# Differential attention with a plain float32 value product, and two query blocks sharing the end of their chain

## The chip, the cores and the metric

The kernel runs on one core of one Trainium2 chip. The metric is the device time of one execution in microseconds (us). A core has five engines that matter here: TensorE (PE, matrix products; PEld is its weight load), VectorE (DVE), ScalarE (ACT), GpSimd (POOL) and SyncE (SP), whose queue issues nearly all DMA transfers. PE writes its results to PSUM, 8 banks of 2 KB for each of 128 partitions; DVE and ACT read them from there, POOL cannot.

## The reference

One encoder layer over 1024 rows of width 1024, in float32: half a SwiGLU step, then two token mixers in parallel (a chunked band attention A with 8 heads, and a differential attention B with 4 heads), gated and merged, then another half SwiGLU step and a norm. The change lies in mixer B:

```python
def diff_attention(q, k, v, t5_table, lam, lambda_init, subln_g):
    ...
    def block(args):
        qblk, bi = args
        ...
        sc = jnp.einsum('bqhrd,bkhrd->bhrqk', qblk, k).astype(jnp.float32) * scale
        ...
        p = jax.nn.softmax(sc, axis=-1)
        attn = p[:, :, 0] - lam * p[:, :, 1]
        return jnp.einsum('bhqk,bkhe->bqhe', attn.astype(v.dtype), v)

    o = lax.map(block, (qblocks, jnp.arange(nqb)))
    o = o.transpose(1, 0, 2, 3, 4).reshape(b, s, h, 2 * d)
    o = rms_norm(o, subln_g) * (1.0 - lambda_init)
    return o.reshape(b, s, h * 2 * d)
```

Each head has two score matrices (r = 0, 1), one value matrix of width 128, and a norm over its 128 outputs. A block of 128 queries sees the keys of its own and earlier chunks.

## The kernel before

**Split products.** PE multiplies operands of type float32r in one pass, at less than float32 accuracy. Almost every product is therefore written as a sum of products of two parts: `split` (L94) rounds a tile to float32r on ACT (`hi`, L97 or, with a scale, L99) and subtracts on DVE (`lo`, L102 or L104), and `mm3` (L126) adds hi x hi, hi x lo and lo x hi. Transposes by PE, and the product at L958, use plain float32 operands.

**Stages.** The first SwiGLU step, then the mixer's input projection (among it `project_v`, L665, which makes the values of both mixers with a seven-product scheme), then both attentions, then the merge, the output projection, and the second SwiGLU step. Intermediate results go through DRAM.

**Projection of the values.** For each of eight results per mixer, `sink` (L673) splits two tiles of 128 rows and 256 columns into hi and lo columns lying side by side, and stores them in `v_d`. For mixer B a head's 256 columns are its 128 hi and its 128 lo columns.

**Attention.** `run` (L811) goes through all jobs, first 32 of A (`jobs_a`), then 32 of B (`jobs_b`: 4 heads of 8 query blocks). A job is a generator: each step of `run` starts one job and moves the four jobs before it to their next `yield`, latest first. A job of B does this:

- Block start: at a head's first job, `load_qkv` (L757) loads queries, keys, exchanged keys and values, 1 MB each, into tiles of the pool `big` (14 buffers, where also the eight outputs `y` of all heads stay). At every second head the bias rows of two heads are loaded too (`bias_rows`, L798, eight DMAs into one tile `nb`).
- Scores for r = 0 and 1 (L779, L780: hi and lo of the keys), bias and row minimum on DVE (L787), exponential and row sum on ACT (L789). Two reciprocals (L922, L924), each into a one-column tile `ri` of a pool with four buffers. L925 makes the weight of the second softmax, L927 the combined probabilities. The first reciprocal, `r1`, is used again at the end.
- Two steps later: up to four 128 x 128 transposes into one PSUM tile `pt` (L795), split into hi and lo (L97, L102).
- One step later: the product with the values. For each block of 128 keys, L943 multiplies the hi probabilities with the 256 columns (hi and lo values), L944 the lo probabilities with the 128 hi columns. ACT scales the two halves by `r1` (L946, L948), POOL adds them (L949). DVE sums the squares (L952), POOL takes the power -1/2 (L139) and scales the identity by it (L955).
- One step later: a plain product of the output with that diagonal transposes and norms it (L958), and `split` with the gain `gsub` (L99, L104) writes the two parts of `y`.

After every second job of B a `filler` (`branch_a`, L881) runs one step: twelve products of 512 columns (L128 to L130) for A's output projection, with a gate tile `gl` loaded from DRAM, one product on DVE (L892) and a store (L893).

The order of each engine's instructions is worked out by the framework from the program's order and its own model of times (`schedule_with_timeline_sim=True`). Each engine, and SP's queue, then keeps that order. A tile that finds no free buffer in its pool waits until one is released.

## Time and profile before

| | |
|---|---|
| time, median of 3 runs | 2154.29 us (2150.46 to 2155.05) |
| span of the profiled execution | 2151.1 us |
| mean granted clock of PE | 0.994 |
| DMA moved in the span | 333.55 MB, mean 155 GB/s |
| stretch of mixer B's softmax and products | from about 1182 to 1353 us |

The page gives the profiled execution by its span, from first to last instruction; the time of a run is taken around it, and the median of the runs is 3.2 us above this span.

How to read the profile: `L943` is line 943 of the kernel. `pv<-vt,whi` names the tile written and those read. A group's row gives line, engine, operation, tiles, shape and count, then the busy time in us and the mean of one in ns, then how long the engine stood idle just before the group's instructions and on whom it waited most. A row of the order of time gives start, duration, engine, line, operation, tiles and count, with the idle time before it in brackets. A row of waits gives who waited for whom, the sum in us, how often, and the longest. Durations of products overlap, since PE takes up the next product while the last one drains, so the pace is read from their starts.

### The profile page before, as it was taken

How to read it: one execution, taken by the hardware profiler on the slowest of the kernel's cores; microseconds unless marked ns; L12 is line 12 of the kernel's file. 1: busy time of each engine (PE TensorE's matmuls, PEld its weight loads, DVE VectorE, ACT ScalarE, POOL GpSimd, SP SyncE). 2: the span in 40 equal slices, each digit the busy share in tenths (PEclk: the TensorE clock that was granted, in tenths of full speed). 3: DMA queues.
4: the chain of work that ended last, by engine and by line, in shares of the span. 5: the costliest groups of instructions: out<-in, count | busy, mean ns of one | idle time of the engine just before them, and what ended most of it. 6: DMA issues, size and time to landing. Idle time of an engine off the chain costs nothing.

```text
span 2151.1 us, 29100 instructions
## 1 busy us (share of the span) xinstructions
PE 2080.7 (97%) x10073; PEld 1738.7 (81%) x10073; DVE 1442.3 (67%) x2650; ACT 980.2 (46%) x1919; POOL 181.4 (8%) x282
## 2 busy tenths in 40 slices
PE   6999999999999999999999988999999999999997
PEld 5788888888888788899788877788788888888886
DVE  7666566677577756566488977558766656658566
ACT  5433333334446544444498665146433333334444
POOL 2120000000001000000066233001000000000001
PEclk9999999999999999999999999999999999999999
DMA  6653333294445544553683364634543333366334
GB/s 194 173 169 111 95 96 120 93 327 143 117 128 162 168 142 164 198 196 136 230 275 105 136 211 133 233 119 151 172 156 95 111 96 95 114 237 228 98 117 158
DMA packets 277555, 333.55 MB, mean 155 GB/s; under 512 B 15404, under 2 KB 167996, under 8 KB 277408
## 3 DMA queue, kind: packets, MB, share of 16 engines
q1 hardware_dynamic: 276080, 327.94, 46.7%
q0 software_dynamic: 1184, 3.24, 0.6%
q8 instruction: 79, 1.29, 0.3%
q14 instruction: 68, 0.56, 0.1%
q10 hardware_dynamic: 144, 0.52, 0.1%
HBM read 226.45 MB, written 105.19 MB: 154 GB/s over the span
## 4 chain that ended last, share of the span: by engine, by line
PE 82%; DVE 6%; DMA 4%; ACT 3%; issue 2%; SPq 1%; POOL 0%; ACTq 0%; DVEq 0%; POOLq 0%
PE prod L128 18%; PE prod L129 18%; PE prod L130 18%; PE po L129 7%; PE po L128 7%; PE po L130 7%; DVE wlo L102 2%; PE pb L128 1%; PE pb L130 1%; PE pb L129 1%; ACT pm L789 1%; DMA raw<-in_ffn_w_in_dram 1%; ACT whi L97 1%; PE tr L205 1%; PE pt L795 1%
## 5 line engine op out<-in xcount | busy, mean ns | idle before, releaser
L129 PE MATMUL po<-wlo,whi 128*128 128x512 f32 x744 | 290.6, 391 | 2.2 <-DVE wlo L102 2.2
L130 PE MATMUL po<-whi,wlo 128*128 128x512 f32 x744 | 289.4, 389 | 0.0
L97 ACT CAST whi<-raw 128x512 fp32r<-128x512 f32 x200 | 124.3, 622 | 308.1 <-PE prod L129 238.3
L97 ACT CAST whi<-B 128x512 fp32r<-128x512 f32 x186 | 115.8, 623 | 272.0 <-PE po L129 265.4
L97 ACT CAST whi<-T 128x512 fp32r<-128x512 f32 x192 | 119.4, 622 | 244.2 <-PE prod L129 224.7
L102 DVE TENSOR_TENSOR wlo<-B,whi 128x512 fp32r<-128x512 f32 x186 | 128.0, 688 | 139.3 <-ACT whi L97 139.2
L113 DVE TENSOR_TENSOR c<-prod,c 128x512 f32<-128x512 f32 x190 | 131.1, 690 | 133.6 <-PE prod L130 121.1
L102 DVE TENSOR_TENSOR wlo<-raw,whi 128x512 fp32r<-128x512 f32 x200 | 137.0, 686 | 106.6 <-ACT whi L97 64.0
L128 PE MATMUL po<-whi 128*128 128x512 f32 x744 | 201.5, 390 | 0.0
L102 DVE TENSOR_TENSOR wlo<-T,whi 128x512 fp32r<-128x512 f32 x192 | 131.8, 687 | 92.1 <-ACT whi L97 90.8
L129 PEld LDWEIGHTS po<-wlo,whi 128*128 128x128 f32 x744 | 139.6, 188 | 33.7 <-DVE wlo L102 5.1
L139 POOL TENSOR_TENSOR r<-v,neg_half 128x1 f32<-128x1 f32 x64 | 49.7, 780 | 1383.0 <-DVE v L180 1264.7
L130 PEld LDWEIGHTS po<-whi,wlo 128*128 128x128 f32 x744 | 139.7, 188 | 28.7
L128 PEld LDWEIGHTS po<-whi 128*128 128x128 f32 x744 | 139.1, 188 | 28.8 <-ACT whi L97 0.2
L102 DVE TENSOR_TENSOR wlo<-N,whi 128x512 fp32r<-128x512 f32 x64 | 44.1, 689 | 113.6 <-PE prod L129 62.9
L102 DVE TENSOR_TENSOR wlo<-ha,whi 128x512 fp32r<-128x512 f32 x154 | 105.4, 684 | 9.0 <-ACT whi L97 9.0
L272 ACT COPY c<-prod 128x512 f32<-128x512 f32 x186 | 103.1, 586 | 11.2 <-DMA hA<-c 4.4
L97 ACT CAST whi<-ha 128x512 fp32r<-128x512 f32 x154 | 94.8, 615 | 16.9 <-PE prod L129 11.4
L789 ACT ACTIVATE pm<-pm,mn 128x640 f32<-128x640 f32 (+7 forms) x128 | 94.0, 736 | 11.8 <-DVE ri L924 6.1
L128 PE MATMUL prod<-S1h,whi 128*128 128x512 f32 x240 | 94.4, 393 | 2.4 <-ACT S1h L97 1.4
L787 DVE CUSTOM_DVE_ANT_0 pm<-sc,nb 128x640 f32<-128x640 f32 (+7 forms) x128 | 87.9, 698 | 11.4 <-PE sc L780 8.8
L128 PE MATMUL prod<-S2h,whi 128*128 128x512 f32 x240 | 94.0, 392 | 1.3 <-ACT whi L97 1.3
(237 smaller groups left out, 5338.9 us busy)
## 6 DMA issues: line engine op xcount, KB each, us to landing
raw<-in_ffn_w_in_dram SPq DMA_DIRECT2D x98, 512.0 KB, 4.3
raw<-in_w_mix_in_dram SPq DMA_DIRECT2D x47, 512.0 KB, 4.4
ha<-hS SPq DMA_DIRECT2D x88, 256.0 KB, 2.6
hA<-c SPq DMA_DIRECT2D x66, 256.0 KB, 4.2
ha<-hA SPq DMA_DIRECT2D x66, 256.0 KB, 2.7
B<-in_ffn_w_out_dram SPq DMA_DIRECT2D x12, 1024.0 KB, 10.2
hS<-hs SPq DMA_DIRECT2D x44, 256.0 KB, 2.7
hS<-c SPq DMA_DIRECT2D x44, 256.0 KB, 4.4
```

The costliest lines, as they stand in the source:

```text
L97: nc.scalar.copy(out=hi, in_=src)
L102: (nc.gpsimd if on_pool else nc.vector).tensor_tensor(out=lo, in0=src, in1=h, op=ALU.subtract)
L113: nc.vector.tensor_tensor(out=out_, in0=a, in1=b, op=op)
L128: nc.tensor.matmul(ps, a[0], b[0], start=first, stop=False, skip_group_check=shared)
L129: nc.tensor.matmul(ps, a[0], b[1], start=False, stop=False, skip_group_check=shared)
L130: nc.tensor.matmul(ps, a[1], b[0], start=False, stop=last, skip_group_check=shared)
L139: nc.gpsimd.tensor_tensor(out=r, in0=v, in1=neg_half, op=ALU.pow)
L205: nc.tensor.transpose(tr[:, k, :], rows[:, k * P:(k + 1) * P], ident)
L272: nc.scalar.copy(out=self.held[name], in_=p)
L787: nc.vector.tensor_tensor_reduce(out=d3, in0=sc, in1=nb.rearrange("p (n w) -> p n w", n=n), scale=1.0, scalar=3e38, op0=ALU.add, op1=ALU.m ...
L789: nc.scalar.activation(out=dst, in_=dst, func=AF.Exp, bias=mn, scale=-1.0, accum_out=rs)
L795: nc.tensor.transpose(pt[:, b, :], p, ident)
```

## The change

The values of mixer B stay plain float32, 128 columns a head, and one tile holds two heads. The transposed probabilities are copied by ACT in place of being split. One plain float32 product per block of keys takes the place of L943 and L944, and one scaling takes the place of L946, L948 and L949. Two consecutive query blocks write their outputs, sums of squares and diagonals into shared tiles; the power, the diagonals, the transposing products and the split run once for the two, in the job of the odd block. The two row sums of a job share a tile, and so do their reciprocals, which are taken in one instruction. The values of a head pair are loaded once, at the pair's first head, behind its keys and ahead of its bias rows, as before; the pair's second head loads none. Mixer A's loads keep their order.

```diff
-    v_d = drams(2, [S, 2 * HALF], "v", F32R)
+    va_d = dram.tile([S, 2 * HALF], F32R, name="va")
+    vb_d = dram.tile([S, HALF], F32, name="vb")
...
                 def sink(th, blk, ap):
+                    t0 = 4 * th + 2 * a
+                    if br == 1:
+                        if (th, blk) == (1, 0):
+                            o = temp([P, 2, 256], "vo")
+                            nc.scalar.copy(out=o, in_=ap)
+                            ap = o
+                        nc.sync.dma_start(out=vb_d[t0 * P:(t0 + 2) * P, blk * 256:(blk + 1) * 256].rearrange(
+                            "(s p) c -> p s c", p=P), in_=ap)
+                        return
...
+        def load_v(src, n, dtype):
+
+            vt = big([P, NT, 256], "vt", dtype)
+            move(nc.sync, vt, src.rearrange("(t p) c -> p t c", p=P)[:, :, n * 256:(n + 1) * 256])
+            return vt
...
-        def transpose_p(blocks):
+        def transpose_p(blocks, whole=False):
...
-            return split_units(pt[:, :len(blocks), :].rearrange("p b q -> p (b q)"))
+            src = pt[:, :len(blocks), :].rearrange("p b q -> p (b q)")
+            if not whole:
+                return split_units(src)
+            dst = sb.tile(list(src.shape), F32, tag="w", bufs=WU, name="pT")
+            nc.scalar.copy(out=dst, in_=src)
+            return dst
...
                     if hb % 2 == 0:
-                        nbs.append(big([P, 2, S], "nb", F32))
+                        nbs.append((big([P, 2, S], "nb", F32), load_v(vb_d, hb // 2, F32)))
                         for hh in range(2):
-                            bias_rows(nbs[-1][:, hh, :], diag_b, hb + hh, EB, WB)
-                    ctx_["nb"] = nbs[-1][:, hb % 2, :]
+                            bias_rows(nbs[-1][0][:, hh, :], diag_b, hb + hh, EB, WB)
+                    ctx_["nb"] = nbs[-1][0][:, hb % 2, :]
+                    ctx_["vt"] = nbs[-1][1][:, :, (hb % 2) * P:(hb % 2 + 1) * P]
...
-                pr, rs = [], []
+                pr, rs = [], small.tile([P, 2], F32, tag="rs2", name="rs2")
...
-                r1, r2 = (small.tile([P, 1], F32, tag="ri", name="ri") for _ in range(2))
-                nc.vector.reciprocal(out=r1, in_=rs[0])
-
-                nc.vector.reciprocal(out=r2, in_=rs[1])
-                nc.vector.scalar_tensor_tensor(out=r2, in0=r2, scalar=neg_lam, in1=rs[0],
+                ri = small.tile([P, 2], F32, tag="ri2", name="ri2")
+                r1, r2 = ri[:, 0:1], ri[:, 1:2]
+                nc.vector.reciprocal(out=ri, in_=rs)
+                nc.vector.scalar_tensor_tensor(out=r2, in0=r2, scalar=neg_lam, in1=rs[:, 0:1],
...
-                pv = ps.tile([P, 256], F32, tag="pv", bufs=2, name="pv")
+                pv = ps.tile([P, P], F32, tag="pv", bufs=2, name="pv")
                 for kb in range(i + 1):
-                    c = slice((kb % 4) * P, (kb % 4 + 1) * P)
-                    pt = pts[kb // 4]
-                    nc.tensor.matmul(pv, pt[0][:, c], vt[:, kb, :], start=kb == 0, stop=False)
-                    nc.tensor.matmul(pv[:, 0:P], pt[1][:, c], vt[:, kb, 0:P], start=False, stop=kb == i)
-                o1 = temp([P, P], "o1")
-                nc.scalar.activation(out=o1, in_=pv[:, P:], func=AF.Copy, scale=r1)
-                o2 = temp([P, P], "o2")
-                nc.scalar.activation(out=o2, in_=pv[:, :P], func=AF.Copy, scale=r1)
-                nc.gpsimd.tensor_tensor(out=o1, in0=o1, in1=o2, op=ALU.add)
...
+                    nc.tensor.matmul(pv, pts[kb // 4][:, (kb % 4) * P:(kb % 4 + 1) * P], vt[:, kb, :],
+                                     start=kb == 0, stop=kb == i)
+                if i % 2 == 0:
+                    ctx_["o"] = temp([P, 2, P], "o"), small.tile([P, 2], F32, tag="v2", bufs=2, name="v2")
+                o, v = ctx_["o"]
+                nc.scalar.activation(out=o[:, i % 2, :], in_=pv, func=AF.Copy, scale=r1)
...
+                if i % 2 == 0:
+                    return
+                r = small.tile([P, 2], F32, tag="r2", bufs=2, name="r2")
+                nc.gpsimd.tensor_tensor(out=r, in0=v, in1=neg_half.to_broadcast([P, 2]), op=ALU.pow)
+                dg = temp([P, 2, P], "dg")
+                for n in range(2):
+                    nc.gpsimd.tensor_tensor(out=dg[:, n, :], in0=ident, in1=r[:, n:n + 1].to_broadcast([P, P]),
+                                            op=ALU.mult)
                 yield
...
+                for n in range(2):
+                    nc.tensor.matmul(tr[:, n, :], o[:, n, :], dg[:, n, :], start=True, stop=True)
+                c = slice((i - 1) * P, (i + 1) * P)
+                split(tr[:, :2, :].rearrange("p b q -> p (b q)"), y[:, 0, c], y[:, 1, c], scale=gsub)
```

More of the change, by code (lines that the diff above doesn't have):

```diff
@@ L673, in sink @@
                 def sink(th, blk, ap):
+                    t0 = 4 * th + 2 * a
[7 more added lines that the diff above has]
+                        return
                     for s in range(2):
                         o = sb.tile([P, HALF], F32R, tag="f", bufs=TF, name="vo")
-                        if br == 0:
-                            hi = bass.AP(o.tensor, o.offset, [o.ap[0], [256, 2], [192, 2], [1, 64]])
-                            lo = bass.AP(o.tensor, o[:, 64:65].offset, [o.ap[0], [256, 2], [64, 2], [1, 64]])
-                            src = ap[:, s, :].rearrange("p (a b d) -> p a b d", a=2, b=2)
-                        else:
-                            hi, lo = (o.rearrange("p (h c d) -> p h c d", h=2, c=2)[:, :, c, :] for c in range(2))
-                            src = ap[:, s, :].rearrange("p (h d) -> p h d", h=2)
+                        hi = bass.AP(o.tensor, o.offset, [o.ap[0], [256, 2], [192, 2], [1, 64]])
+                        lo = bass.AP(o.tensor, o[:, 64:65].offset, [o.ap[0], [256, 2], [64, 2], [1, 64]])
+                        src = ap[:, s, :].rearrange("p (a b d) -> p a b d", a=2, b=2)
                         split(src, hi, lo)
-                        t = 4 * th + 2 * a + s
-                        move(nc.sync, v_d[br][t * P:(t + 1) * P, blk * HALF:(blk + 1) * HALF], o)
+                        move(nc.sync, va_d[(t0 + s) * P:(t0 + s + 1) * P, blk * HALF:(blk + 1) * HALF], o)
                 return sink
@@ L824, in job @@
                     ctx_["qkv"] = load_qkv(pr)
+                    ctx_["vt"] = load_v(va_d, pr, F32R)
                     ctx_["y"] = big([P, 2, S], "y")
@@ L829, in job @@
                         bias_rows(ctx_["nb"][:, hh, :WA], diag_a, 2 * pr + hh, EA, WA)
-                qkv, y, nb = (ctx_[n] for n in ("qkv", "y", "nb"))
-                vt = qkv[3]
+                qkv, vt, y, nb = (ctx_[n] for n in ("qkv", "vt", "y", "nb"))
                 i0, i1 = 2 * sb_, 2 * sb_ + 1
@@ L932, in job @@
                 for b0 in range(0, i + 1, 4):
-                    pts.append(transpose_p([pr[0][:, b * P:(b + 1) * P] for b in range(b0, min(b0 + 4, i + 1))]))
+                    pts.append(transpose_p([pr[0][:, b * P:(b + 1) * P] for b in range(b0, min(b0 + 4, i + 1))], True))
                 due[0] += 0.5
@@ L945, in job @@
-                o1 = temp([P, P], "o1")
-                nc.scalar.activation(out=o1, in_=pv[:, P:], func=AF.Copy, scale=r1)
-                o2 = temp([P, P], "o2")
-                nc.scalar.activation(out=o2, in_=pv[:, :P], func=AF.Copy, scale=r1)
-                nc.gpsimd.tensor_tensor(out=o1, in0=o1, in1=o2, op=ALU.add)
-                sq = temp([P, P], "sq")
-                v = small.tile([P, 1], F32, tag="v", name="v")
-                nc.vector.tensor_tensor_reduce(out=sq, in0=o1, in1=o1, scale=1.0 / P, scalar=EPS,
-                                               op0=ALU.mult, op1=ALU.add, accum_out=v)
@@ L954, in job @@
-                dg = small.tile([P, P], F32, tag="dg", bufs=2, name="dg")
-                nc.gpsimd.tensor_tensor(out=dg, in0=ident, in1=rsqrt(v).to_broadcast([P, P]), op=ALU.mult)
+                    nc.tensor.matmul(pv, pts[kb // 4][:, (kb % 4) * P:(kb % 4 + 1) * P], vt[:, kb, :],
[3 more added lines that the diff above has]
+                o, v = ctx_["o"]
@@ new lines, in job @@
+                nc.scalar.activation(out=o[:, i % 2, :], in_=pv, func=AF.Copy, scale=r1)
+                sq = small.tile([P, P], F32, tag="sq", bufs=1, name="sq")
+                nc.vector.tensor_tensor_reduce(out=sq, in0=o[:, i % 2, :], in1=o[:, i % 2, :], scale=1.0 / P,
+                                               scalar=EPS, op0=ALU.mult, op1=ALU.add,
+                                               accum_out=v[:, i % 2:i % 2 + 1])
+                if i % 2 == 0:
+                    return
@@ L956, in job @@
+                r = small.tile([P, 2], F32, tag="r2", bufs=2, name="r2")
[4 more added lines that the diff above has]
+                                            op=ALU.mult)
                 yield
                 tr = ps.tile([P, 4, P], F32, tag="pt", bufs=2, name="try")
-                nc.tensor.matmul(tr[:, 0, :], o1, dg, start=True, stop=True)
@@ L959, in job @@
-                c = slice(i * P, (i + 1) * P)
-                split(tr[:, 0, :], y[:, 0, c], y[:, 1, c], scale=gsub)
+                for n in range(2):
+                    nc.tensor.matmul(tr[:, n, :], o[:, n, :], dg[:, n, :], start=True, stop=True)
+                c = slice((i - 1) * P, (i + 1) * P)
+                split(tr[:, :2, :].rearrange("p b q -> p (b q)"), y[:, 0, c], y[:, 1, c], scale=gsub)
             return [job(i) for i in range(NT)]
```

13 lines of the change are left out of this document (4 added, 9 removed).

## The prediction

> **What bounds the kernel now.** I read the page first, then the busy time by stretch, then the groups, the order of time and the waits of the one stage that the edits reach.
>
> ```profile
> span 2151.1 us, 29100 instructions
> PE 2080.7 (97%) x10073; PEld 1738.7 (81%) x10073; DVE 1442.3 (67%) x2650; ACT 980.2 (46%) x1919; POOL 181.4 (8%) x282
> ```
>
> TensorE (PE) is busy 97% of the span, so what is left to gain lies where it is not. Busy time by stretch (columns: stretch, its length, then busy time and instructions of PE, weight loads, DVE, ACT, POOL, the granted clock, DMA):
>
> ```profile
> 908.00:955.00 47.00, 47.00 (x331) 44.19 (x330) 30.33 (x54) 20.26 (x41) 0.00 (x0) 1.00 0.49 164
> 1188.00:1229.00 41.00, 38.59 (x236) 33.56 (x235) 37.73 (x118) 28.00 (x77) 12.56 (x22) 1.00 0.47 168
> 1229.00:1270.00 41.00, 35.17 (x208) 30.63 (x208) 32.17 (x102) 25.91 (x70) 14.30 (x26) 0.96 0.61 192
> 1270.00:1312.00 42.00, 39.27 (x231) 33.88 (x230) 33.88 (x107) 25.68 (x71) 13.60 (x24) 0.96 0.45 163
> 1312.00:1353.00 41.00, 31.37 (x188) 26.52 (x186) 28.20 (x81) 22.24 (x58) 15.12 (x28) 0.96 0.48 156
> ```
>
> The first row lies in the projection of the values, where PE is busy without a break. The other four are the four heads of the differential attention, 165 us in all. There DVE is busy 132.0 us of 165 (92% in the first head), PE 144.4, and the clock falls below 1 in three heads. Busy PE counts latency, so I need PE's pace, from the order of time:
>
> ```profile
> 1250.35 0.33 PE L943 MATMUL pv<-vt,whi 128*128 128x256 f32 x1
> 1250.52 0.22 PE L944 MATMUL pv<-vt,wlo 128*128 128x128 f32 x1
> 1250.58 0.34 PE L943 MATMUL pv<-vt,whi 128*128 128x256 f32 x1
> 1302.88 0.38 PE L958 MATMUL try<-dg,o 128*128 128x128 f32 x2
> 1263.56 1.04 PE L795 MATMUL pt<-ident,pm 128*128 128x128 f32 x8
> 1268.36 0.39 PE L129 MATMUL pb<-y,whi 128*128 128x512 f32 x1
> 1268.59 0.39 PE L130 MATMUL pb<-y,wlo 128*128 128x512 f32 x1
> ```
>
> Starts tell the pace: a pair of value products is 0.23 us (1250.35 to 1250.58), 512 columns 0.23 as well (1268.36 to 1268.59), a transpose (1.04-0.27)/7 = 0.11. One head has 36 pairs (8.3 us), 36 transposes (4.0), scores of 18432 columns (36 at 0.23: 8.3), 45 products of the filler (10.3), and the 8 plain products of L958 (16 records at 0.11: 1.8). That is 32.7 us of PE work in 41 us. So about 8 us per head, 34 in all, are waiting or half clock. A mean clock of 0.96 over 41 us is 41 x 0.04 = 1.6 us of lost work, in three heads 5 us. The rest is waits:
>
> ```profile
> 1236.86 0.52 SPq L124 DMA_DIRECT2D vt<-v  x1
> 1237.47 14.33 SPq L805 DMA_DIRECT2D nb<-diag_b  x8
> 1205.74 1.23 DVE L787 CUSTOM_DVE_ANT_0 pm<-sc,nb 128x1024 f32<-128x1024 f32 x1 [0.45 <-PE sc L780]
> 1208.73 0.29 DVE L787 CUSTOM_DVE_ANT_0 pm<-sc,nb 128x128 f32<-128x128 f32 x1 [0.91 <-PE sc L780]
> 1237.18 1.22 DVE L787 CUSTOM_DVE_ANT_0 pm<-sc,nb 128x1024 f32<-128x1024 f32 x1
> 1253.23 0.29 DVE L787 CUSTOM_DVE_ANT_0 pm<-sc,nb 128x128 f32<-128x128 f32 x1 [1.99 <-DMA nb<-diag_b]
> 1281.59 1.22 DVE L787 CUSTOM_DVE_ANT_0 pm<-sc,nb 128x1024 f32<-128x1024 f32 x1
> 1294.49 0.29 DVE L787 CUSTOM_DVE_ANT_0 pm<-sc,nb 128x128 f32<-128x128 f32 x1 [0.78 <-PE sc L780]
> vt<-v SPq DMA_DIRECT2D x1, 1024.0 KB, 14.6
> SPq L805 <- DMA vt<-v: 4.4, 1, 4.4
> DVE ri L924 <- ACT o L948: 6.1, 5, 2.7
> PEld try L958 <- POOL dg L955: 6.8, 6, 2.3
> 1335.66 0.36 PE L943 MATMUL pv<-vt,whi 128*128 128x256 f32 x1 [2.83 <-DVE gl L892]
> 1348.71 0.22 PE L944 MATMUL pv<-vt,wlo 128*128 128x128 f32 x1
> 1353.03 0.50 PE L128 MATMUL pb<-y,whi 128*128 128x512 f32 x1 [0.84 <-DVE y L104]
> ```
>
> Each head's last softmax has 1024 columns, its first 128. Between the first two heads lie 1.8 us (1207.0 to 1208.7). Between the last softmax of the second head (ends 1238.4) and the first of the third lie 14.8 us, because the new head's operands and bias rows are still landing; between third and fourth (1282.8 to 1294.5) 11.7 us. At the end, 4.3 us pass from the last value product to the next stage's first.
>
> **The change part by part.** The groups that it touches, over the four heads:
>
> ```profile
> L102 DVE TENSOR_TENSOR wlo<-pt,whi 128x512 fp32r<-128x512 f32 (+3 forms) x48 | 26.3, 551 | 7.4 <-ACT whi L97 7.3
> L104 DVE SCALAR_TENSOR_TENSOR y<-try,gsub,y 128x128 fp32r<-128x128 f32 x32 | 11.0, 343 | 6.1 <-ACT y L99 5.9
> L924 DVE RECIPROCAL ri<-rs 128x1 f32<-128x1 f32 x30 | 4.7, 156 | 6.2 <-ACT o L948 6.1
> L948 ACT ACTIVATE o<-pv,ri 128x128 f32<-128x128 f32 x32 | 11.7, 365 | 0.0
> L139 POOL TENSOR_TENSOR r<-v,neg_half 128x1 f32<-128x1 f32 x32 | 23.6, 737 | 40.6 <-DVE v L952 34.3 <-DVE ri L924 4.0 <-PE try L958 1.5
> L949 POOL TENSOR_TENSOR o<-o,o 128x128 f32<-128x128 f32 x32 | 14.7, 460 | 62.6 <-ACT o L948 62.6
> L955 POOL TENSOR_TENSOR dg<-ident,r 128x128 f32<-128x128 f32 x32 | 15.9, 498 | 2.4
> L102 DVE TENSOR_TENSOR wlo<-pt,whi 128x256 fp32r<-128x256 f32 x8 | 3.3, 415 | 0.0
> L102 DVE TENSOR_TENSOR wlo<-pt,whi 128x128 fp32r<-128x128 f32 x8 | 2.3, 288 | 1.8 <-ACT whi L97 1.7
> L97 ACT CAST vo<-c x24: 399/406/408, 913.2 to 993.9; 128x256 fp32r<-128x256 f32 x24
> ```
>
> *Value product.* Each pair (256 and 128 columns) becomes one plain float32 product of 128 columns. The trace has plain products in L958: each is two records 0.11 apart, so 0.22 against 0.23 for the pair. 144 of them change PE's work by -1.4 us; I take 0. The bounds: 0.22 if they follow each other as L958's two records do, and two whole records after each other, 2 x (0.38-0.11) = 0.54, if each waits for its predecessor's end (144 x 0.31 = +45 us). I take the near row. The Trainium skill, page "FP8 and Floating Point Precision", section "TensorE Precision Notes", says that true FP32 takes four passes through the array, which speaks against this edit: four times 128 columns where the pair streams 384. By columns alone, with 0.23 us for 512, the pair would be 0.17 us and the change would add 144 x 0.06 = 8.6 us of PE work; the trace does not bear that out, since the pair already takes 0.23.
>
> *Split of the transposed probabilities.* The 48 subtractions on DVE go: 26.3 us. The ACT conversion becomes an ACT copy of the same shape, counted equal. A product now waits for ACT alone.
>
> *Output chain.* L948 goes (ACT -11.7 us), L949 goes (POOL -14.7), half of L139 goes (POOL -11.8). Sixteen double-width splits replace 32: by the widths 128 and 256 of L102, 288 and 415 ns, the wide form costs 127 ns more, so 16 x 470 = 7.5 in place of 11.0 on DVE (-3.5). One reciprocal of two goes (-5.0 for 32). DVE in all: 26.3 + 3.5 + 5.0 = 34.8 of 132.0 us, 8.7 per head. That brings it to 97 us, or 24 per head, below PE's 32.7.
>
> *Waits that change.* The reciprocal L924 waits for an earlier block's L948, since two one-column tiles a block share four buffers and the first is held until the output is scaled. One two-column tile a block gives a block more of slack: 6.1 us of DVE stops, with the exponentials behind them. An even block's output now waits for the odd one; behind that queue the two products of L958 and the wide split on PE, ACT and DVE, while the following scores and transposes do not need it. Only at a head's end does somebody wait: the last chain loses L948 (0.37) and L949 (0.46) and gains a diagonal (0.50), a product (0.22) and two wide forms (0.13 each by the widths above). That is +0.15; I take 0, bounds -1 and +1.
>
> *Loads.* Two 1 MB value loads go (second and fourth head), the last of four loads there. In the third head the value load stays ahead of the bias rows on SP: there the eight issues took 14.33 us, to 1251.8, and 4.4 us of that SP stood until the value load had landed (1236.86 + 14.6 = 1251.5). So this boundary's 14.8 us stay, and I take only the PE work that DVE and POOL let slip into it. The fourth head's keys share the DMA engines with one load fewer of four; the values of that head are in SBUF already.
>
> *Projection of the values.* Half of 32 ACT conversions of 0.4 us and as many DVE subtractions go (the row shows the 24 that read an SBUF tile), 16 stores become 8, and two ACT copies come. PE is busy 47.0 of 47.0 us there, so I cost it at 0. It would be worth up to 1 us either way if PE's cover were missing.
>
> **The sum**, on the profiled execution's 2151.1 us span (3.2 us under the median of 2154.29, which I take as what lies around it, unchanged):
> - first head, where DVE was 92% busy: 41 to 37, -4 (bounds 0 and -8, PE's 32.7);
> - second boundary, its load order unchanged: -1 (+2 and -4);
> - third boundary, one load fewer and less half clock: -2 (0 and -3);
> - reciprocal ring: -2 (0 and -6);
> - last head, the 2.8 us stop behind L892, part of the waits for the diagonal (6.8 us on the weight side), half clock: -3 (+1 and -6).
>
> Sum -12 us (bounds +3 and -27): span 2139, time 2142. What is late next is the load of a head's keys, which the previous head's last scores still release, and PE's own work.
>
> **The rivals.**
> 1. *The boundaries set the pace, so DVE's relief is absorbed.* For it: 14.8 and 11.7 us without softmax, and loads that cannot start earlier, since ten or more of 14 large buffers stay held. Against it: the first head has a boundary of 1.8 us and takes 41 us all the same, with DVE at 92%. It gives -2: 2152. Chance 0.15.
> 2. *Plain products do not follow each other at 0.11 us a record in an accumulating row.* Place: the 144 products. Price: up to 144 x 0.31 = 45 us, less the 12 gained: 2187. It makes the kernel slower from a cadence of 0.23 + 12/144 = 0.31 us. Against it: L958's records and the transposes at 0.11. Chance 0.04.
> 3. *The order that the planner works out anew puts a load later at a boundary.* A boundary of 15 us that becomes 35 outweighs the gains: 2160. For it: one boundary is 1.8 us and another 14.8 in the same code, so where a load falls in SP's order matters. Chance 0.06.
> 4. *PE pays by columns* (+8.6 us, -12 + 8.6): 2151. Against it: the pair at 0.23. Chance 0.03. The four-pass rule of the Trainium skill, named above, would give this one.
> 5. *PE becomes gapless*, all bounds met: 2127. Chance 0.10.
>
> **How the numbers follow.** The forecast has 0.62: 2142. About 0.2% (4.3 us) is what a measurement of this kernel can tell from no change. Faster by more: 0.62 + 0.10 and 0.03 of the first rival, 0.75; within: the rest of that rival and the fourth, 0.15; slower: 0.04 + 0.06 = 0.10. The range 2127 to 2154 takes in the bounds of the five terms and the first rival; below and above it lie 0.2.
>
> **What would show it.** Right: DVE near 97 us in the stage, no subtraction of the transposed tile, plain products 0.22 apart, each head 36 to 40 us, the stretch from 1188 about 12 us shorter, all else within a us. Wrong: plain products over 0.3 apart; every head still about 41 us with PE idle at the boundaries and DVE relaxed; a boundary well over 15 us.

## The result, and the profile after

The changed kernel takes 2132.59 us (median of 4 runs, 2130.75 to 2134.11) against 2154.32 us (4 runs, 2150.46 to 2155.05) for the kernel before, measured beside it. The ratio is 0.9904, with a 95% interval of 0.989 to 0.9918: about 21 us less. The predicted 2142 lies 9 us above it, inside the range 2127 to 2154.

The head of the page after:

```profile
span 2131.0 us, 28800 instructions
...
PE 2071.2 (97%) x10073; PEld 1734.1 (81%) x10073; DVE 1411.5 (66%) x2538; ACT 966.1 (45%) x1857; POOL 159.8 (7%) x234
```

PE still runs 10073 instructions and is busy 97%. DVE has lost 112 instructions, ACT 62, POOL 48. The span is 20.1 us shorter, and PE's busy time fell by 9.5 us of these, though its number of instructions is the same.

Busy time by stretch, after (columns as in the prediction: stretch, length, PE, weight loads, DVE, ACT, POOL, granted clock, DMA). The first row lies in the projection of the values, right behind the stretch that the prediction shows; the next four are the four heads, the last is the whole stage:

```profile
955.00:1004.00 49.00, 49.00 (x373) 47.29 (x372) 23.46 (x37) 16.96 (x30) 0.00 (x0) 1.00 0.35 115
...
1188.00:1223.00 35.00, 34.16 (x220) 30.11 (x219) 29.50 (x87) 24.16 (x63) 6.28 (x10) 1.00 0.47 166
1223.00:1257.00 34.00, 31.53 (x208) 28.24 (x207) 23.43 (x71) 20.60 (x50) 6.52 (x14) 1.00 0.65 216
1257.00:1296.00 39.00, 35.93 (x232) 31.91 (x232) 29.85 (x92) 23.84 (x64) 8.60 (x12) 1.00 0.49 162
1296.00:1334.00 38.00, 33.24 (x212) 29.16 (x211) 24.76 (x69) 21.58 (x51) 10.63 (x16) 1.00 0.46 151
...
1188.00:1334.00 146.00, 134.86 (x866) 119.41 (x865) 107.54 (x315) 90.18 (x226) 32.03 (x52) 1.00 0.52 173
```

And the whole stage in the kernel before, in the same columns:

```profile
1188.00:1353.00 165.00, 144.40 (x855) 124.59 (x853) 131.98 (x406) 101.83 (x274) 55.59 (x100) 0.97 0.50 170
```

165 us became 146. PE without a record: 20.6 us before (165 - 144.4), 11.1 after, so 9.5 less. The clock went from 0.97 to 1.00, which is some 5 us of work (0.03 x 165) in this pair of profiles. The remaining 4 to 5 us lie inside busy records, whose durations count more than the pace (0.33 us for a record of L943, 0.17 us to the next start); which records those are, the rows do not tell. From the first softmax of the stage to the next stage's first product it is 171.0 us before and 150.5 after, 20.5 less: all of the gain is in this stage. From the next stage's first product to the end it is 798.1 us before and 797.1 after; the way to the stage took 1.4 us longer.

The 5 us of clock are not a steady part of the gain. A second profile of the same changed kernel (e11 below) shows its stage at 0.98, and its third head at 0.92:

```profile
1188.00:1336.00 148.00, 137.20 (x860) 121.29 (x859) 107.11 (x315) 90.48 (x226) 31.97 (x52) 0.98 0.52 170
```

Over all executions the mean granted clock of the whole kernel is 0.9937 before (41 executions) and 0.9944 after (8). That is an estimated 1 to 2 us of work (0.0007 x 2150).

The pace of the new product, from the order of time:

```profile
1222.40 1.05 PE L952 MATMUL pv<-vt,pT 128*128 128x128 f32 x8
1223.21 0.47 PE L788 MATMUL sc<-ks,qs 128*128 128x512 f32 x1
```

Eight records, which are four products, in 1.05 us: (1.05 - 0.27)/7 = 0.11 us a record, 0.22 a product, as L958 had it before. The groups of the stage after:

```profile
L952 PE MATMUL pv<-vt,pT 128*128 128x128 f32 x288 | 39.2, 277 | 1.5 <-DVE gl L906 1.0 <-ACT o L957 0.5
...
L104 DVE SCALAR_TENSOR_TENSOR y<-try,gsub,y 128x256 fp32r<-128x256 f32 x16 | 7.6, 477 | 2.7 <-ACT y L99 2.7
L935 DVE RECIPROCAL ri<-rs 128x2 f32<-128x2 f32 x30 | 4.8, 161 | 8.3 <-ACT pm L798 8.3
```

288 records replace 288, and PE stood 1.5 us before them. The wide split takes 7.6 us, the shared reciprocal 161 ns against 156 for one column. The reciprocal no longer waits for an output's scaling (6.1 us before) but for the exponential whose sum it needs. The waits of the stage, after (engine, line, releaser: us in total, times, longest):

```profile
DVE ri L935 <- ACT pm L798: 8.3, 11, 2.1
...
PEld try L973 <- POOL dg L968: 2.2, 1, 2.2
...
PEld pt L804 <- ACT pT L809: 1.7, 4, 0.7
...
PEld pv L952 <- ACT pT L809: 0.6, 2, 0.3
```

The weight side's wait for the diagonal fell from 6.8 us in six places to 2.2 in one, which is the end of the last head. The last two rows are what PE still waits for the copy that replaced conversion and subtraction. Last, the boundaries and the end of the stage, from the order of time after (last softmax of a head, 1024 columns; first of the next, 128):

```profile
1206.90 1.22 DVE L796 CUSTOM_DVE_ANT_0 pm<-sc,nb 128x1024 f32<-128x1024 f32 x1
1213.48 0.28 DVE L796 CUSTOM_DVE_ANT_0 pm<-sc,nb 128x128 f32<-128x128 f32 x1
...
1241.60 1.22 DVE L796 CUSTOM_DVE_ANT_0 pm<-sc,nb 128x1024 f32<-128x1024 f32 x1
1254.02 0.29 DVE L796 CUSTOM_DVE_ANT_0 pm<-sc,nb 128x128 f32<-128x128 f32 x1 [2.03 <-DMA nb<-diag_b]
...
1270.44 0.43 SPq L124 DMA_DIRECT2D qs<-q  x1
...
1271.51 0.50 SPq L119 DMA_DIRECT2D gl<-g  x1
...
1282.12 0.69 DVE L906 TENSOR_TENSOR gl<-pb,gl 128x512 f32<-128x512 f32 x1 [3.52 <-DMA gl<-g]
...
1283.27 0.39 SPq L124 DMA_DIRECT2D kl<-kx  x1
...
1284.01 0.33 PE L788 MATMUL sc<-ks,qs 128*128 128x128 f32 x1 [2.46 <-DVE mn L796]
...
1285.39 1.22 DVE L796 CUSTOM_DVE_ANT_0 pm<-sc,nb 128x1024 f32<-128x1024 f32 x1
1290.28 0.28 DVE L796 CUSTOM_DVE_ANT_0 pm<-sc,nb 128x128 f32<-128x128 f32 x1
...
1328.76 1.17 PE L952 MATMUL pv<-vt,pT 128*128 128x128 f32 x9
1331.96 0.85 PE L973 MATMUL try<-dg,o 128*128 128x128 f32 x4 [2.04 <-POOL dg L968]
1333.89 0.50 PE L128 MATMUL pb<-y,whi 128*128 128x512 f32 x1 [1.08 <-DVE y L104]
```

The stretch without softmax is now 5.4, 11.2 and 3.7 us at the three boundaries; it was 1.8, 14.8 and 11.7. The second still ends on a bias row. At the third, the last head's queries and keys were issued from 1270.44 on, some 15 us ahead of the previous head's last softmax; before, they were issued just ahead of it:

```profile
1280.59 0.42 SPq L124 DMA_DIRECT2D qs<-q  x1
...
1281.62 0.44 SPq L124 DMA_DIRECT2D kl<-kx  x1
```

The exchanged keys (`kl`), the last operand that the scores need, were still issued late, at 1283.27. But with the other two already there, they landed 5.6 us after their issue, against 11.4 before.

The early issue had a price too. The filler's gate tile, 256 KB, was issued at 1271.51 right behind these two loads of 1 MB and took 10.5 us to land, against a median of 4.1 for its 20 loads in the stage. DVE stood 3.5 us for it, the softmax behind it came late, and PE stood 2.5 us for that. The same happened at 1327 in the last head, where the gate tile landed behind weight loads and DVE stood 4.0 us. All such waits in the stage, after the change:

```profile
L906 DVE TENSOR_TENSOR gl<-pb,gl 128x512 f32<-128x512 f32 x16 | 11.0, 686 | 10.2 <-DMA gl<-g 9.6 <-PE pb L130 0.6
```

Before, DVE stood 4.0 us for gate tiles.

### The profile page after: what moved, and what is told of

Read it like the earlier page. It is cut to its first block, busy times and chain, and to the rows that moved or that the text cites. A ratio compares the mean times of both kernels' runs of the same rounds, so it can differ in the third digit from the quotient of the medians.

```text
span 2131.0 us, 28800 instructions
## 1 busy us (share of the span) xinstructions
PE 2071.2 (97%) x10073; PEld 1734.1 (81%) x10073; DVE 1411.5 (66%) x2538; ACT 966.1 (45%) x1857; POOL 159.8 (7%) x234
## 4 chain that ended last, share of the span: by engine, by line
PE 83%; DVE 6%; DMA 5%; issue 3%; ACT 3%; SPq 0%; POOL 0%; ACTq 0%; DVEq 0%; POOLq 0%
PE prod L128 18%; PE prod L129 18%; PE prod L130 18%; PE po L129 7%; PE po L128 7%; PE po L130 7%; DVE wlo L102 2%; DMA gl<-g 1%; PE tr L205 1%; PE pb L128 1%; PE pb L129 1%; PE pb L130 1%; ACT pm L798 1%; ACT whi L97 1%; DMA ha<-hS 1%
## 5 line engine op out<-in xcount | busy, mean ns | idle before, releaser
L139 POOL TENSOR_TENSOR r<-v,neg_half 128x1 f32<-128x1 f32 x32 | 28.0, 880 | 1339.9 <-DVE v L180 1262.4
L97 ACT CAST whi<-ha 128x512 fp32r<-128x512 f32 x154 | 94.8, 616 | 16.9 <-PE prod L129 11.4
## 6 DMA issues: line engine op xcount, KB each, us to landing
B<-in_ffn_w_out_dram SPq DMA_DIRECT2D x12, 1024.0 KB, 10.2
```

The source lines that it names most:

```text
L97: nc.scalar.copy(out=hi, in_=src)
L139: nc.gpsimd.tensor_tensor(out=r, in0=v, in1=neg_half, op=ALU.pow)
```

## The experiments

Each was measured beside the kernel before. "Saves" is (1 - ratio) x 2154.3 us; an interval is some 2 to 3.5 us to each side. "Stage" is, from one profile, the time from the first softmax of the stage to the next stage's first product. The two profiles of the changed kernel (after and e11) differ by 2.9 us in it, and the profiled executions of e2, e5 and e14 lie 3 to 4 us from their medians, so differences of that size in this column say little.

| kernel | median us | ratio, 95% interval | saves | stage us |
|---|---|---|---|---|
| before | 2154.3 | 1 | 0 | 171.0 |
| e1: before, shared reciprocal alone | 2148.25 | 0.9979 (0.997 to 0.9988) | 4.5 | 164.8 |
| e5: before, pairing alone | 2139.35 | 0.9935 (0.9923 to 0.9948) | 14.0 | 159.6 |
| e2: plain product alone | 2138.75 | 0.9931 (0.9918 to 0.9945) | 14.9 | 152.1 |
| e3: plain product and reciprocal, no pairing | 2128.42 | 0.9884 (0.9871 to 0.9896) | 25.0 | 145.2 |
| after, all three | 2132.59 | 0.9904 (0.989 to 0.9918) | 20.7 | 150.5 |
| e11: after, once more | 2134.65 | 0.9907 (0.9893 to 0.992) | 20.0 | 153.4 |
| e4: after, subtractions back | 2137.15 | 0.9925 (0.9913 to 0.9937) | 16.2 | 154.4 |
| e6: e3, values loaded at every head | 2129.19 | 0.988 (0.9867 to 0.9894) | 25.9 | 145.4 |
| e7: e3, bias rows before the values | 2126.8 | 0.9877 (0.986 to 0.9893) | 26.5 | 147.3 |
| e9: e3, scaling and addition back | 2134.3 | 0.9905 (0.9891 to 0.9918) | 20.5 | 150.0 |
| e10: e3, DVE behind the copy, both waits | 2143.72 | 0.995 (0.9937 to 0.9962) | 10.8 | 162.1 |
| e15: e3, product waits for DVE | 2138.85 | 0.9929 (0.9916 to 0.9941) | 15.3 | 153.5 |
| e14: e3, DVE reads the PSUM tile | 2150.88 | 0.9984 (0.9975 to 0.9993) | 3.4 | 165.6 |

**The change taken apart.** First each of its three parts by itself. The shared reciprocal in the kernel before:

```diff
-                pr, rs = [], []
+                pr, rs = [], small.tile([P, 2], F32, tag="rs2", name="rs2")
...
-                r1, r2 = (small.tile([P, 1], F32, tag="ri", name="ri") for _ in range(2))
-                nc.vector.reciprocal(out=r1, in_=rs[0])
-
-                nc.vector.reciprocal(out=r2, in_=rs[1])
+                ri = small.tile([P, 2], F32, tag="ri2", name="ri2")
+                r1, r2 = ri[:, 0:1], ri[:, 1:2]
+                nc.vector.reciprocal(out=ri, in_=rs)
...
```

> The kernel before, with only the shared two-column tiles for row sums and reciprocals and one reciprocal a job; products, splits, pairing and loads as before. Theory 'DVE load' (the stage was held by DVE, 132 of 165 us busy, and the gain is its 34.8 us less of work): DVE loses only 5 us of work, so -2 to -4 us against before (2150 to 2152). Theory 'waits' (the gain is the waits that went: reciprocal behind an earlier block's output, product behind the subtraction, addition on POOL): the ring is one of three such waits and frees 6 us of DVE stops, so -6 to -9 us. Planner's order as cause: no fixed sign.

It saves 4.5 us, between what the two theories expected, so it decides neither. An estimated 3 us of these are clock (a mean of 0.9953 over its executions, 0.9939 for the kernel before beside it).

The pairing in the kernel before, with its pairs of products, both scalings and the addition kept:

```diff
-                o1 = temp([P, P], "o1")
+                if i % 2 == 0:
+                    ctx_["o"] = temp([P, 2, P], "o"), small.tile([P, 2], F32, tag="v2", bufs=2, name="v2")
+                o, v = ctx_["o"]
+                o1 = o[:, i % 2, :]
...
+                if i % 2 == 0:
+                    return
+                r = small.tile([P, 2], F32, tag="r2", bufs=2, name="r2")
+                nc.gpsimd.tensor_tensor(out=r, in0=v, in1=neg_half.to_broadcast([P, 2]), op=ALU.pow)
...
-                split(tr[:, 0, :], y[:, 0, c], y[:, 1, c], scale=gsub)
...
+                split(tr[:, :2, :].rearrange("p b q -> p (b q)"), y[:, 0, c], y[:, 1, c], scale=gsub)
```

> The kernel before with the pairing alone: hi and lo products, both scalings and the addition stay; power, diagonals, transposing products and split run once for two blocks. Theory 'fewer steps gain': DVE -3.5, ACT -4, POOL -12 us of work and half the PSUM tiles for the transposed output, -3 to -8 us against before. Theory 'pairing costs' (the run without it was 4 us faster than the whole change; the first block's output waits a step for the second): 0 to +6 us.

It saves 14.0 us, more than either theory expected, where I had costed the pairing at nothing.

The plain product without the other two (against the changed kernel, the reciprocals and the unpaired output of the kernel before are put back; values once per pair of heads, the ACT copy and the single scaling stay):

```diff
-                pr, rs = [], small.tile([P, 2], F32, tag="rs2", name="rs2")
+                pr, rs = [], []
...
-                nc.vector.reciprocal(out=ri, in_=rs)
...
+                nc.vector.reciprocal(out=r1, in_=rs[0])
+
+                nc.vector.reciprocal(out=r2, in_=rs[1])
...
-                if i % 2 == 0:
-                    ctx_["o"] = temp([P, 2, P], "o"), small.tile([P, 2], F32, tag="v2", bufs=2, name="v2")
...
+                o = temp([P, P], "o")
+                nc.scalar.activation(out=o, in_=pv, func=AF.Copy, scale=r1)
...
-                split(tr[:, :2, :].rearrange("p b q -> p (b q)"), y[:, 0, c], y[:, 1, c], scale=gsub)
...
+                split(tr[:, 0, :], y[:, 0, c], y[:, 1, c], scale=gsub)
```

> The change without the shared row sums and reciprocals and without the pairing of two blocks: plain product, plain values with one load per head pair, one ACT copy for a split, one scaling of the output. Theory 'DVE load': 26 of 35 us of DVE relief remain, so -14 to -18 us against before. Theory 'waits': the ring wait is back and its DVE stops with it, so -8 to -12 us. Rival 'pairing' (fewer, larger steps on POOL, ACT and DVE are the gain): under -8 us.

It saves 14.9 us, as theory 'DVE load' expected and more than 'waits' did. The old ring's wait is still there, in its list of waits:

```profile
DVE ri L938 <- ACT o L958: 4.8, 6, 1.5
```

Then the changed kernel without the pairing alone (the last two hunks of the diff above):

> The change without the pairing: each block has its own power, diagonal, transposing product and split. DVE gets 3.5 us of work back, ACT about 4, POOL 12. Theory 'DVE load': -18 to -21 us against before. Theory 'waits': the same, the chain per block is short without the addition on POOL. Rival 'pairing': -10 to -14 us.

It saves 25.0 us, more than every theory expected, and its median is 4 us below the changed kernel's. The whole stage of e3 by busy time, and its DVE group of the gate tile:

```profile
1188.00:1328.00 140.00, 134.74 (x869) 120.08 (x867) 110.11 (x334) 92.78 (x242) 35.90 (x67) 1.00 0.53 175
```

```profile
L906 DVE TENSOR_TENSOR gl<-pb,gl 128x512 f32<-128x512 f32 x16 | 10.9, 682 | 1.6 <-PE pb L130 1.5
```

PE has no record for 5.3 us of 140, against 11.1 of 146 in the changed kernel, and DVE never stands for a gate tile, against 9.6 us there. Three things follow. The parts do not add: alone they save 4.5 + 14.0 + 14.9 = 33.4, together 20.7; a likely reason, not shown, is that they take away some of the same stops of PE. The reciprocal is worth 10.1 us once the products are plain (25.0 - 14.9), twice what it is worth alone. And the pairing saves 14 us in the kernel before, but costs 4 to 5 us beside the other two. The changed kernel measured once more bears that out:

> The whole change again, beside the others of this call. If pairing costs what the run without it showed: ratio near 0.990, about 4 us above 0.988 of that run; if that was the day's chip: 0.988.

It saves 20.0 us, as the first time (20.7); e3, e6 and e7, all without pairing, save 25.0 to 26.5. The intervals of e3 and of the changed kernel still touch (0.9871 to 0.9896, 0.989 to 0.9918); it is the five runs together that tell the two kinds apart.

**DVE's load.** The 48 subtractions put back into the changed kernel, into a tile that nobody reads; no product waits for them:

```diff
             nc.scalar.copy(out=dst, in_=src)
+            lo = unit(list(src.shape), "lo")
+            nc.vector.tensor_tensor(out=lo, in0=src, in1=dst, op=ALU.subtract)
```

> The change with the 48 subtractions of the transposed tile put back on DVE, into a tile that nobody reads: 26 us of DVE work are back and no product waits for them; only the PSUM tile and the buffer are held until they are done. Theory 'DVE load': most of the gain goes, -4 to -9 us against before. Theory 'waits': the gain stays, -17 to -21 us.

The stage's row and the group that was added, of this run:

```profile
1188.00:1338.00 150.00, 138.96 (x865) 121.58 (x865) 126.77 (x363) 90.86 (x226) 29.59 (x52) 0.99 0.51 173
```

```profile
L811 DVE TENSOR_TENSOR lo<-pt,pT 128x512 fp32r<-128x512 f32 (+3 forms) x48 | 25.9, 549 | 1.8 <-ACT pT L809 1.6
```

DVE is busy 126.8 of 150 us, 85%, with 25.9 us of the old subtraction in it, and the PSUM tile is held until DVE has read it. That costs 4 to 4.5 us of the gain (20.0 and 20.7 less 16.2), far from what theory 'DVE load' expected and just under the range of 'waits'. So DVE's busy time itself is a small part of the 20 us, as far as one new order of the planner can tell.

**The loads.** In e3, the values loaded anew at each head, as before the change, with the bias rows still once per pair:

```diff
                     ctx_["qkv"] = load_qkv(4 + hb)
+                    ctx_["v"] = load_v(vb_d, hb // 2, F32)
...
-                    ctx_["vt"] = nbs[-1][1][:, :, (hb % 2) * P:(hb % 2 + 1) * P]
+                    ctx_["vt"] = ctx_["v"][:, :, (hb % 2) * P:(hb % 2 + 1) * P]
```

> The change without pairing (2128.4 us, -24.7 against before), but the 1 MB of a head pair's values is loaded anew at every head, behind its keys, so that four loads and a large buffer per head stand as before the change. Theory 'waits': the fewer loads carry little, -21 to -25 us. Theory 'loads' (buffers and DMA at the boundaries are what got better): the third boundary goes back from about 7 us toward 12 and half clock returns, -14 to -19 us.

25.9 against 25.0: two 1 MB loads more cost nothing that can be told, as theory 'waits' expected. In this run the last head's queries were also issued early, at 1271.4, and the exchanged keys again landed 5.6 us after their issue, with the value load behind them. So the shorter boundary is not owed to the load that fell away. That the planner's order on SP brought the queries forward is the likely reason.

In e3, the bias rows issued ahead of the values:

```diff
-                        nbs.append((big([P, 2, S], "nb", F32), load_v(vb_d, hb // 2, F32)))
+                        nbt = big([P, 2, S], "nb", F32)
                         for hh in range(2):
-                            bias_rows(nbs[-1][0][:, hh, :], diag_b, hb + hh, EB, WB)
+                            bias_rows(nbt[:, hh, :], diag_b, hb + hh, EB, WB)
+                        nbs.append((nbt, load_v(vb_d, hb // 2, F32)))
```

> The change without pairing, with the bias rows issued ahead of the value load in the first and third head. If the second boundary (12.5 us, PE 2.0 us idle behind the bias rows) is set by rows that wait for the value load: softmax starts 3 to 5 us sooner there and the time falls by 2 to 4 us, to 2124 to 2126. If it is set by the keys: no difference, 2127 to 2130. If the values then come too late: up to 2134.

The second boundary in e3, and in e7:

```profile
1239.46 1.21 DVE L796 CUSTOM_DVE_ANT_0 pm<-sc,nb 128x1024 f32<-128x1024 f32 x1
...
1253.21 0.29 DVE L796 CUSTOM_DVE_ANT_0 pm<-sc,nb 128x128 f32<-128x128 f32 x1 [1.82 <-DMA nb<-diag_b]
```

```profile
1241.82 1.22 DVE L796 CUSTOM_DVE_ANT_0 pm<-sc,nb 128x1024 f32<-128x1024 f32 x1
...
1245.78 0.29 DVE L796 CUSTOM_DVE_ANT_0 pm<-sc,nb 128x128 f32<-128x128 f32 x1 [1.54 <-DMA nb<-diag_b]
```

The stretch without softmax shrinks from 12.5 us to 2.7, and the time stays the same within the intervals (0.9877 and 0.9884). By itself this settles little, because the new order also opened a stretch of 6.0 us at the first boundary, where e3 has none; over the three boundaries only 3.8 us went (19.5 to 15.7). For the head with this boundary, PE's lost time (the interval less an estimate of the PE work in it, worked out in the next section) fell from 4.5 to 2.8 us. So the stretch has a price, but far below its length, since PE has the previous head's transposes, products and its filler to do meanwhile. Over all fourteen profiles PE loses an estimated 2 to 6 us in this head where the stretch is up to 12.5 us, and 4 to 10 where it is 14.8 or more. e7 has the lowest median of all, between the two ranges that were expected, but cannot be told from e3.

**The output's chain.** In e3, the second scaling on ACT and the addition on POOL are put back (the sum is now twice the output, and the norm behind it takes the factor out again):

```diff
+                o2 = temp([P, P], "o2")
+                nc.scalar.activation(out=o2, in_=pv, func=AF.Copy, scale=r1)
+                nc.gpsimd.tensor_tensor(out=o, in0=o, in1=o2, op=ALU.add)
```

> The change without pairing, with a second scaling of the output on ACT and the addition on POOL put back (the output is twice as large, and the norm takes that out again): ACT gets 11.7 us and POOL 14.7 us of work back and the chain behind the product 0.8 us per block. Theory 'waits' with the output chain as a main part: 6 to 10 us of the 24.7 go. Theory 'waits' with the subtraction behind the product as the main part: 1 to 4 us go. Theory 'DVE load': 0 to 2.

4.5 us of the gain go (25.0 - 20.5), between the two ranges of 'waits'. The waits show where the chain is longer:

```profile
POOL o L958 <- ACT o L957: 54.4, 22, 5.2
...
DVE sq L961 <- POOL o L958: 9.3, 8, 2.2
```

POOL's long wait costs nothing by itself. But DVE now stops 9.3 us for POOL's sum, ahead of the next softmax in its queue.

**The product's wait for DVE.** Before the change, a value product waited for ACT's conversion and DVE's subtraction, and the PSUM tile of the transposes was held by both. Three small DVE steps behind the ACT copy put these waits back. Both of them (DVE writes one column of the copy again, from PSUM):

```diff
             nc.scalar.copy(out=dst, in_=src)
+            nc.vector.tensor_copy(out=dst[:, 0:1], in_=src[:, 0:1])
```

> The change without pairing; behind ACT's copy of each transposed tile, DVE writes one column of it anew (the same numbers), so that the products wait for DVE's turn again, for about 4 us of DVE work. Theory 'waits': 5 to 10 us of the 24.7 go, and PE's products wait on DVE. Theory 'DVE load': at most 2 us go.

Its group, and waits of its stage:

```profile
L810 DVE COPY pT<-pt 128x1 f32<-128x1 f32 x48 | 7.3, 151 | 11.4 <-ACT pT L809 11.4
```

```profile
PE try L965 <- DVE pT L810: 6.0, 7, 2.7
...
PEld pt L804 <- DVE pT L810: 4.4, 3, 2.4
```

48 copies of 0.15 us, 7.3 us of DVE in all, cost 14 us of the 25, more than any theory expected. DVE stands 11.4 us for ACT's copy with the following softmaxes behind it, and PE stands for DVE where it wants the PSUM tile back.

The product's wait alone (DVE rewrites the column from the copy itself, in SBUF, so PSUM is free after ACT):

```diff
             nc.scalar.copy(out=dst, in_=src)
+            nc.vector.tensor_copy(out=dst[:, 0:1], in_=dst[:, 0:1])
```

> The change without pairing; DVE rewrites one column of ACT's copy in SBUF, in place. The PSUM tile is free as soon as ACT has copied it, but every product waits for DVE's turn. Theory 'turn': 10 to 15 us of the 25 go. Theory 'hold': 0 to 4 us go.

```profile
DVE pT L810 <- ACT pT L809: 8.9, 11, 1.9
...
PEld sc L788 <- DVE mn L796: 4.0, 7, 1.5
...
PEld pv L953 <- DVE pT L810: 1.8, 4, 0.6
```

About 10 us go (25.0 - 15.3), just under the range of theory 'turn'. PE's weight loads wait directly for the rewritten column only 1.8 us; they wait longer for a softmax (4.0, against 2.3 in e3). DVE itself stands 8.9 us for ACT's copy, with the following softmaxes behind it. So the run does not separate two causes: the product that waits for DVE, and DVE that waits in its queue.

The PSUM tile's hold alone (DVE reads the column into a tile that nobody uses):

```diff
             nc.scalar.copy(out=dst, in_=src)
+            one = small.tile([P, 1], F32, tag="one", bufs=2, name="one")
+            nc.vector.tensor_copy(out=one, in_=src[:, 0:1])
```

> The change without pairing; DVE reads one column of each transposed tile from PSUM into a tile that nobody uses, behind ACT's copy. The products wait for ACT alone, but the PSUM tile (two buffers, shared with the transposing product of the output) is held until DVE's turn. The run with both the hold and the products' wait lost 13 to 15 us of 25. Theory 'hold': 10 to 15 us go here, and the next run loses 0 to 4. Theory 'turn' (the products' wait for DVE): 0 to 4 us go here.

This run asks less than e10 does and loses more: 21.6 us, outside every theory. It also sits badly with e4, which holds the same tile for DVE, longer, and loses 4 to 4.5 (e4 has the pairing, so the transposed outputs take half as many of the shared tiles). So its loss is hardly the price of the hold. A wait of its stage, and one place of it in the order of time:

```profile
PE pv L954 <- ACT pT L809: 10.2, 14, 2.5
```

```profile
1202.87 1.16 PE L954 MATMUL pv<-vt,pT 128*128 128x128 f32 x8 [1.55 <-ACT pT L809]
```

PE waits 10.2 us for ACT's copy, which no edit touched and for which the changed kernel's weight loads wait 0.6 us: the products stand too close behind their transposes. From the end of a block's last transposes to the first product on them pass 1.56 us (median of the 32 blocks, from the records), with 8.5 PE instructions between; in e3 it is 1.98 us with 16, in the changed kernel 2.55 with 18. The planner gave this program another order, and these 10.2 us are about half of what was lost. That the order is the cause is argued from these rows; no run held the order fixed.

## Why the prediction was right, and where not

**The sum.** Terms of a head, taken from last value product to last value product (the first from its first value product), from the records:

| term | predicted | measured | without moved PE work (estimate) |
|---|---|---|---|
| first head | -4 (0 to -8) | 40.5 to 33.3, -7.2 | -2.6 |
| second boundary and head | -1 (+2 to -4) | 41.3 to 34.2, -7.1 | -6.3 |
| third boundary and head | -2 (0 to -3) | 42.0 to 38.3, -3.7 | -2.7 |
| last head | -3 (+1 to -6) | 36.4 to 34.0, -2.4 | -7.8 |
| reciprocal ring, spread over the heads | -2 (0 to -6) | -4.5 alone, -10.1 beside the plain product | (lies in the heads) |
| sum | -12 (+3 to -27) | -20.5 | -19.4 |

The sums are of the unrounded terms. The last column is needed because the heads do not hold equal PE work, as the prediction's 32.7 us for each had it. The planner also moved work between them. By the counts of the records the filler's products were 48, 45, 51 and 36 in the four intervals and became 44, 40, 48 and 48; the score products 66, 40, 53 and 19 became 46, 44, 52 and 36. At the paces of the trace (0.227 us for 512 columns, others by their columns, 0.11 for each narrow record, 0.23 for a pair) that is an estimated 36, 31, 35 and 26 us of work before, and 31, 31, 34 and 31 after. What is left of each interval is time in which PE stood or ran slowly: 4.8, 9.9, 7.1 and 10.3 us before, 2.2, 3.6, 4.3 and 2.5 after.

The sign, the stage and the mechanism in outline (PE's stops go, its work stays) held; how much of the gain is half clock differs from execution to execution. The size was 9 us short: the second boundary, the last head and the reciprocals were put too small, and the pairing at nothing. The first head's -4, the largest term, met a fall of 2.6 us in PE's lost time; its other 4.6 us are work that went to other heads. The range has a slip of its own: the bounds of the five terms reach +3, which is 2157, and not 2154.

**The plain product at no change** was right: 0.11 us a record, 0.22 a product, PE's count of records the same. The Trainium skill, page "FP8 and Floating Point Precision", section "TensorE Precision Notes", gives true FP32 four passes. The trace is in line with it for the plain product, 0.22 us for 128 columns beside 0.23 for 512 float32r ones, but does not show it. The product has two weight loads, which start 0.112 us apart (median), and these alone give 0.22 too. Columns do not give the old pair's time: 384 of them would be 0.17, and it took 0.23. Its two weight loads start 0.11 and 0.12 us apart, which does give 0.23:

```profile
1250.30 0.19 PEld L943 LDWEIGHTS pv<-vt,whi 128*128 128x128 f32 x1
1250.41 0.19 PEld L944 LDWEIGHTS pv<-vt,wlo 128*128 128x128 f32 x1
```

So the 8.6 us of the fourth rival did not come.

**The second boundary and the last head were the terms furthest off**: -1 against -7.1 (-6.3 without the moved work), and -3 against an estimated -7.8 without it. At the second boundary the observation was right, since the gap stayed (11.2 us, ended by a bias row, against 14.8). The step from it put too much on the gap, as if PE could gain little while it stays: PE lost an estimated 9.9 us in this head before and 3.6 after, with a gap only 3.6 us shorter. Some 1.6 us of that is half clock (0.04 x 41), which this profile after lacks. The last head lost 10.3 us before and 2.5 after; the prediction saw its stops (the 2.8 us behind L892, the diagonal, half clock) and took 3 us of them. The first rival, whose price was these gaps, did not come: 2132.6 against its 2152.

**The reciprocal ring was mis-sized**, -2 against -4.5 alone and -10.1 beside the plain product. The prediction saw the 6.1 us wait and took 2 us of it. Part of the 10.1 is clock: the mean granted clock is 0.9960 over e3's four executions and 0.9933 over e2's six, an estimated 5 to 6 us (0.0027 x 2140).

**The pairing costed at nothing** was wrong in both directions: -14 by itself, +4 to +5 beside the other two. "Only at a head's end does somebody wait" was right as a reading of the waits, for what remains is one wait of 2.0 us there, and the tail is 4.2 us long, against 4.3 before and 3.6 in e3 (1326.5 to 1330.1). That explains 0.6 us of the 4 to 5 that it costs. The rest lies in the heads, where PE does the same work in both and loses an estimated 12.7 us in the changed kernel against 8.0 in e3. The third head has 3.0 of this difference and the last 1.2, and there stand the two longest waits for the gate tile (3.5 and 4.0 us; in e11, the same program, 3.9 and 4.2; in e3 none). So what the pairing costs beside the other two looks like the price of one order of loads rather than of the pairing; no run held the order fixed to show it. How a pairing saves 14 us in the kernel before, no run tells.

**DVE at 97 us** did not come: 107.5. The subtraction took 34.8 us of group times off a busy time. Group times are sums of records, and records overlap, as these three of the changed kernel do:

```profile
1288.13 0.22 DVE L936 SCALAR_TENSOR_TENSOR ri<-ri,neg_lam,rs 128x1 f32<-128x1 f32 x1
1288.26 0.29 DVE L959 CUSTOM_DVE_ANT_0 sq<-o 128x128 f32<-128x128 f32 x1
1288.47 1.28 DVE L938 SCALAR_TENSOR_TENSOR pm<-pm,ri 128x1024 f32<-128x1024 f32 x1
```

Each begins 0.08 to 0.09 us before the one ahead of it ends. Summed over the stage, DVE's groups fell from 157.5 to 124.8 us, 32.7, near the 34.8; its busy time, which counts an overlap once, fell by 24.4. The difference of 8.3 us is about 0.09 us for each of the 91 instructions that went (406 - 315). And "DVE below PE's 32.7 a head" was not the lever: in e4, DVE is back at 126.8 us and 16 of the 20 us remain. What counts more is where DVE's steps stand in the chain: 48 short ones behind ACT's copy and ahead of the products cost about 10 us (e15), although here too the planner's order is not held fixed.

**The loads and the projection of the values at nothing**: right. e6 shows no price for two loads more; PE is busy 49.0 of 49.0 us in the projection. **The third rival**, a load put later by the planner's new order, came in part. At the third boundary it went the other way: the last head's queries came 10 us earlier (1280.6 to 1270.4), and the boundary went from 11.7 to 3.7 us (6.1 in e11, so some of that is chance). But the gate tile behind them came late, which the rival did not name. **The fifth rival's** 2127 is where e3 and e7 arrive (2128.4 and 2126.8), not the change as made; PE is not without gaps there, since e3 has 5.3 us without a PE record left.

What stays open: how much of each difference between these runs is the edit, and how much the order that the planner works out anew for every program. e14 against e10 suggests that the latter can be 7 us or more (21.6 - 14.2).

## What to carry to other kernels

When an engine is near its limit beside PE, look first at where its steps stand in the chain to PE's operands, and only then at its share of busy time: 26 us of DVE work that no product waited for cost 4 us, and 48 short steps of 0.15 us between ACT's copy and the products cost 10 to 14, in orders that the planner made anew each time. Measure the parts of a change singly and left out singly, since here a part that saved 14 us alone cost 4 to 5 us beside the others, and the version without it has the lower time, 2128 us. When a planner makes the order, look after each change for a small load that now stands behind large ones. A stretch in which one engine's stage stands still can cost PE far less than its length, where PE has other work in it: here an estimated 1.7 us for 9.8 (e7 against e3).

## What was not expected of the hardware

A plain float32 product of 128 columns keeps PE no longer than the two float32r products that stood for it (0.22 and 0.23 us), so the splitting of these operands bought nothing on PE and cost a subtraction on DVE. Half clock comes and goes between executions of one program: the first profile of the changed kernel has none inside the stage, the second a stretch of 6.8 us at 1282.3, and the kernel before three of 3.4 us each (at 1254.6, 1285.3 and 1336.5). One profile of each kernel therefore does not show what a change does to the clock. A load of 256 KB issued just behind two of 1 MB took 10.5 us to land, against a median of 4.1.
